# First-half retention: the last 128 queries of each head read a 384-token state in place of three score blocks

## The chip, the cores and the metric

The kernel runs on one core of a Trainium2 chip. The metric is the device time of one execution in microseconds (us). Before the change three runs took 1643.71, 1645.24 and 1647.24 us; their median, 1645.24, is the time before.

## The reference: what is computed

Two layers over 1024 tokens of width 1024, in float32. Layer 0 is a retention layer with 4 heads (queries and keys of 256 values, values of 512), layer 1 a stick-breaking attention. The change concerns the retention alone, for which the reference says, per head with decay gamma,

```
o_t = sum over s <= t of gamma^(t-s) (q_t . k_s) v_s
```

and which it computes in chunks of 128 tokens: scores inside a chunk, and a state (the decayed sum of k_j v_j^T over all earlier chunks, 256 x 512 values) for what lies ahead of the chunk. Each row of o is then normalised to mean 0 and variance 1 over its 512 values, multiplied by a gate and projected.

## The kernel before, in words

**Precision.** Each float32 operand is held as two numbers of the matmul format, a high part and the rest. `split` makes them: ACT copies the source (high part), DVE subtracts that copy from the source (low part). A product is a triple of matmuls, `mm3`: high x high, high x low, low x high. ACT, DVE and PE therefore see one, one and three instructions for each tile.

**Retention, tiled.** The tokens are two halves (t = 0 and 1) of 512, each four blocks of 128. The decay is put on values and normalisation constants when they are loaded, so that scores and states need no decay table. A unit `AHead(t, h)` is one head on one half. In `scores`, `fetch` loads q, k and v in eight loads and splits each; `score(jb)` multiplies key block jb with the queries from block jb on, 512, 384, 256 or 128 wide, in two halves of the 256 dimensions, so six matmuls into one PSUM tile `pz`; the result is split into `sc` and its diagonal block masked on POOL. For t = 0, `kt(tb)` also transposes the keys of a block (four PE transposes and one ACT copy, tile `vo`).

In `mix`, `o(ib)` sums, for query block ib, one triple for each key block up to it (tile `po`), then takes statistics on DVE, three small operations on POOL and one normalising ACT operation (`sgn`) that reads `po` last; that ACT operation of block ib is issued with block ib + 1. For t = 0, `state_out(d)` multiplies the transposed keys of all four blocks with the values (four triples for each half d of the dimensions), scales, splits (`ko`) and stores the state; for t = 1, `state_in` loads it and each o starts with two triples of queries with state. `gate` multiplies with the gate and transposes.

**Tiles and order.** PSUM has eight banks: two each for `pma`, `pmb`, `pz` and `po`. SBUF tiles of like size share groups of buffers: `b` (28 buffers; among them `ko`, `v` and the wide scores) and `f` (25; raw weights `wraw`, `f`, `sg`, `vo` and the narrow scores). Nothing runs in the order in which it is written: `merge` interleaves a main list (projection chunks) with side lists (the scores of the next head, the mix of this one), every operation is recorded (line 229), and `Plan` then sets the order on each engine by a list schedule with costs for operations, loads and buffers. All loads and stores go through SP's queue, in order. The first half's head 0 runs beside the last chunks of the gate projection, heads 1 to 3 beside the output projection of the head before.

## Time and profile before

| | |
|---|---|
| median of three runs | 1645.24 us |
| the profiled execution | 1644.4 us, span 1642.7 us |
| PE busy | 1625.7 us (99% of the span), 7638 matmuls |
| DVE, ACT, POOL busy | 1259.9, 806.6, 253.1 us |
| mean granted PE clock | 0.998 |
| the first-half heads | from about 450 to 612 us of the span |

The times of a timeline row are its start from the beginning of the span and its length. A PE row's length includes the pipeline's drain, so rows overlap: what a group costs is the start of the next row less its own. Every operation has line 229 (the recorder), so tiles tell them apart: `pz`, `po`, `pma`, `pmb` are PSUM tiles, `whl` split weights, `wraw` weights as loaded, `ko` split q, k or state, `vo` transposed keys, `oT` and `qk` inputs of the output projection.

### The profile page before, as it was taken

To read this page: it belongs to the slowest core of one execution; us is meant where nothing else is said; L and a number is where in the kernel's file an instruction comes from. 1 tells how busy PE (TensorE), PEld (TensorE's weight loads), DVE (VectorE), ACT (ScalarE), POOL (GpSimd) and SP (SyncE) were. 2 spreads that over 40 slices of the span, in tenths; PEclk is the share of its full clock that TensorE was granted. 3 is DMA by queue.
4 is the path that set the end of the run, shared out by engine and by line. 5 is a ranking of instruction groups with operands and counts; after the bars stand their busy time and mean duration, and the time that the engine had idled before them with its cause. 6 is when DMAs were issued, how large, how long until landed. Compare 5 with 4: busy or idle time off the path is not lost.

```text
span 1642.7 us, 23070 instructions
## 1 busy us (share of the span) xinstructions
PE 1625.7 (99%) x7638; PEld 1351.8 (82%) x7638; DVE 1259.9 (77%) x1955; ACT 806.6 (49%) x1480; POOL 253.1 (15%) x339
## 2 busy tenths in 40 slices
PE   8999999999999999999999999999999999999997
PEld 7888888888888888888878888888888888888886
DVE  6998679795775667777999677756747887778997
ACT  7633432322665445533665454545555655545643
POOL 0000024230022113451300000000002221212510
PEclk9999999999999999999999999999999999999999
DMA  7675636486567787788667686657686878787894
GB/s 277 238 247 176 224 117 217 154 299 219 188 232 260 249 281 257 256 296 293 213 212 266 259 301 210 249 167 253 221 319 215 277 239 301 275 283 258 279 305 150
DMA packets 196824, 399.60 MB, mean 243 GB/s; under 512 B 22112, under 2 KB 22752, under 8 KB 196704
## 3 DMA queue, kind: packets, MB, share of 16 engines
q1 hardware_dynamic: 196704, 398.12, 70.5%
q8 instruction: 60, 0.98, 0.3%
q14 instruction: 60, 0.49, 0.1%
HBM read 282.69 MB, written 115.34 MB: 242 GB/s over the span
## 4 chain that ended last, share of the span: by engine, by line
PE 77%; DVE 2%; issue 1%; ACT 0%; POOLq 0%; DVEq 0%; POOL 0%
PE po L229 20%; PE pma L229 20%; PE pmb L229 20%; PE pz L229 17%; DVE f L229 1%; DVE S L229 0%; DVE whl L229 0%; DVE wraw L229 0%; DVE acc L229 0%; POOLq L1762 0%; DVEq L1762 0%; ACT qk L229 0%; POOL col L229 0%; ACT whl L229 0%; DVE small L229 0%
## 5 line engine op out<-in xcount | busy, mean ns | idle before, releaser
L229 ACT ACTIVATE whl<-wraw 128x512 fp32r<-128x512 f32 (+1 forms) x392 | 233.3, 626 | 312.4 <-PE pmb L229 105.0
L229 DVE TENSOR_TENSOR whl<-wraw,whl 128x512 fp32r<-128x512 f32 x392 | 281.8, 742 | 135.0 <-ACT whl L229 134.3
L229 PE MATMUL pmb<-oT,whl 128*128 128x512 f32 x552 | 142.9, 394 | 0.0
L229 PE MATMUL pma<-oT,whl 128*128 128x512 f32 x552 | 140.2, 394 | 0.0
L229 PE MATMUL pma<-whl,xh 128*128 128x512 f32 x456 | 118.5, 393 | 1.0 <-DVE whl L229 0.9
L229 PE MATMUL pmb<-whl,xh 128*128 128x512 f32 x456 | 118.0, 393 | 0.9 <-ACT f L229 0.9
L229 PEld LDWEIGHTS pma<-oT,whl 128*128 128x128 f32 x552 | 101.7, 188 | 20.4
L229 PEld LDWEIGHTS pmb<-oT,whl 128*128 128x128 f32 x552 | 101.2, 188 | 19.3
L229 POOL TENSOR_SCALAR_AFFINE_SELECT f<-f 128x128 f32<-128x128 f32 x64 | 31.3, 504 | 527.8 <-DMA wraw<-in_wts_dram 416.1
L229 PE MATMUL pz<-ko,ko 128*128 128x512 f32 (+3 forms) x480 | 103.9, 338 | 0.0
L229 PEld LDWEIGHTS pmb<-whl,xh 128*128 128x128 f32 x456 | 86.1, 189 | 19.9 <-ACT f L229 1.5
L229 PEld LDWEIGHTS pma<-whl,xh 128*128 128x128 f32 x456 | 85.6, 189 | 19.7 <-DVE whl L229 1.7
L229 PE MATMUL pma<-xh,whl 128*128 128x512 f32 x384 | 99.1, 392 | 0.0
L229 PE MATMUL pmb<-xh,whl 128*128 128x512 f32 x384 | 98.6, 390 | 0.0
L229 POOL TENSOR_TENSOR f<-f,f 128x512 f32<-128x512 f32 x32 | 51.0, 1604 | 253.7 <-DVE f L229 224.3
L229 PEld LDWEIGHTS pz<-ko,ko 128*128 128x128 f32 x480 | 78.4, 189 | 9.5 <-DVE AT L229 0.7
L229 PE MATMUL pz<-xh,whl 128*128 128x512 f32 x336 | 85.2, 389 | 0.0
L229 PE MATMUL po<-xh,whl 128*128 128x512 f32 x336 | 85.2, 389 | 0.0
L229 PEld LDWEIGHTS pmb<-xh,whl 128*128 128x128 f32 x384 | 71.8, 188 | 14.9
L229 PEld LDWEIGHTS pma<-xh,whl 128*128 128x128 f32 x384 | 71.4, 188 | 14.8 <-issue 0.2
L229 DVE SCALAR_TENSOR_TENSOR wraw<-wraw,gn,wraw 128x512 f32<-128x512 f32 x96 | 71.3, 757 | 14.3 <-ACT wraw L229 6.2
L229 ACT ACTIVATE AT<-pz 128x512 fp32r<-128x512 f32 (+1 forms) x96 | 45.9, 491 | 66.4 <-PE pz L229 64.9
(197 smaller groups left out, 3380.6 us busy)
## 6 DMA issues: line engine op xcount, KB each, us to landing
wraw<-in_wts_dram SPq DMA_DIRECT2D x559, 256.0 KB, 5.2
v<-v SPq DMA_DIRECT2D x64, 512.0 KB, 6.6
y<-f SPq DMA_DIRECT2D x112, 256.0 KB, 3.0
f<-y SPq DMA_DIRECT2D x88, 256.0 KB, 4.2
ko<-kq SPq DMA_DIRECT2D x40, 512.0 KB, 5.7
kq<-v SPq DMA_DIRECT2D x32, 512.0 KB, 6.0
av<-f SPq DMA_DIRECT2D x32, 256.0 KB, 2.7
ag<-sg SPq DMA_DIRECT2D x32, 256.0 KB, 2.7
```

The lines of the kernel that those rows point to most:

```text
L229: f(*[_real(a) for a in o.args], **{k: _real(v) for k, v in o.kw.items()})
```

## The change: what it does

For t = 0 the fourth query block (ib = 3) no longer multiplies with key blocks 0, 1 and 2. Scores lose those columns: widths 384, 256, 128 and 128 in place of 512, 384, 256 and 128. `kt` is now interleaved with `score`. After o(0), `state_part(d)` forms the state of blocks 0 to 2 (three triples a half), copies it to SBUF (`f`) and splits it (`ko`); o(3) takes two triples of queries with that state and one of its own scores. `state_out(d)` multiplies block 3 alone, adds the kept copy on DVE, then scales, splits and stores. The 256-wide and the 128-wide scores now share one tag in group `f`. The second half is as it was.

```diff
             def score(jb):
-                w = 512 - 128 * jb
+                w = 512 - 128 * jb if self.t else max(384 - 128 * jb, 128)
                 p = PS("z")
                 jl = slice(128 * jb, 128 * jb + 128)
                 for d in range(2):
-                    mm3(p[:, :w], k[d][:, 0, jl], k[d][:, 1, jl], q[d][:, 0, 128 * jb:], q[d][:, 1, 128 * jb:], d == 0, d == 1)
-                s = S(f"sc{jb}", [2, w], F32R)
+                    mm3(p[:, :w], k[d][:, 0, jl], k[d][:, 1, jl], q[d][:, 0, 128 * jb:128 * jb + w], q[d][:, 1, 128 * jb:128 * jb + w], d == 0, d == 1)
+                s = S(f"sc{jb}" if w > 256 else "sc2", [2, w], F32R)
...
-            st = [lambda jb=jb: score(jb) for jb in range(4)]
-            if self.t == 0:
-                st += [lambda tb=tb: kt(tb) for tb in range(4)]
-            return st
+            if self.t:
+                return [lambda jb=jb: score(jb) for jb in range(4)]
+            return [lambda f=f, b=b: f(b) for b in range(4) for f in (score, kt)]
...
+            def products(d, blocks):
+                p = PS("o")
+                for tb in blocks:
+                    n, kn, v = slice(128 * d, 128 * d + 128), self.kn[tb], self.v[tb]
+                    mm3(p[:], kn[:, 0, n], kn[:, 1, n], v[:, 0, :], v[:, 1, :], tb == blocks[0], tb == blocks[-1])
+                return p
+
+            def state_part(d):
+                p = products(d, (0, 1, 2))
+                f, s = S("f2", [512]), hl("ko")
+                A_.activation(f[:], p[:], AF.Copy)
+                split((s[:, 0, :], s[:, 1, :]), f[:])
+                self.part.append(f)
+                self.state.append(s)
 
             def state_out(d):
-                p = PS("o")
-                for tb in range(4):
-                    n, kn, v = slice(128 * d, 128 * d + 128), self.kn[tb], self.v[tb]
-                    mm3(p[:], kn[:, 0, n], kn[:, 1, n], v[:, 0, :], v[:, 1, :], tb == 0, tb == 3)
-                s = hl("ko")
-                gg = GAMMA[h] ** HT
-                A_.activation(s[:, 0, :], p[:], AF.Copy, scale=gg)
-                V.scalar_tensor_tensor(s[:, 1, :], p[:], gg, f32(s[:, 0, :]), ALU.mult, ALU.subtract)
+                p = products(d, (3,))
+                f, s = self.part[d], hl("ko")
+                V.tensor_tensor(f[:], p[:], f[:], ALU.add)
+                split((s[:, 0, :], s[:, 1, :]), f[:], GAMMA[h] ** HT)
                 dma(st_d[h][d][:], flat(s))
...
                 il = slice(128 * ib, 128 * ib + 128)
-                for d, s in enumerate(self.state):
+                blocks = range(ib + 1) if self.t or ib < 3 else (3,)
+                state = self.state if self.t or ib == 3 else []
+                for d, s in enumerate(state):
                     mm3(p[:], q[d][:, 0, il], q[d][:, 1, il], s[:, 0, :], s[:, 1, :], d == 0, False)
-                for jb in range(ib + 1):
+                for jb in blocks:
                     n = slice(128 * (ib - jb), 128 * (ib - jb) + 128)
                     sc, v = self.sc[jb], self.v[jb]
-                    mm3(p[:], sc[:, 0, n], sc[:, 1, n], v[:, 0, :], v[:, 1, :], not self.state and jb == 0, jb == ib)
+                    mm3(p[:], sc[:, 0, n], sc[:, 1, n], v[:, 0, :], v[:, 1, :], not state and jb == 0, jb == ib)
...
             if self.t == 0:
                 self.give = [lambda d=d: state_out(d) for d in range(2)]
-                return os
+                return os[:1] + [lambda d=d: state_part(d) for d in range(2)] + os[1:]
```

Where `Plan` puts this shows in the order on the engines. PE, head 0, before: o(2) (`po721`), o(3) (`po728`), two score groups of head 1, a projection chunk and the first state half (`po743`).

```order
L229 MATMUL po721_4516<-v651_4069,sc2664_4312 128x512 x3
L229 MATMUL po728_4539<-v647_4061,sc0660_4259 128x512 x3
L229 MATMUL po728_4539<-v649_4053,sc1662_4274 128x512 x3
L229 MATMUL po728_4539<-v651_4069,sc2664_4312 128x512 x3
L229 MATMUL po728_4539<-v653_4100,sc3666_4320 128x512 x3
L229 MATMUL pz736_4576<-ko684_4167,ko688_4182 128x256 x3
L229 MATMUL pz736_4576<-ko686_4175,ko690_4190 128x256 x3
```

PE, head 0, after, from the last triple of the second partial state (`po712`) to o(2)'s start; `pz715` and `pz717` are scores and transposed keys of head 1.

```order
L229 MATMUL po712_4454<-v651_4069,vo673_4334 128x512 x3
L229 MATMUL pz715_4441<-ko686_4250,ko690_4295 128x384
L229 MATMUL pz717_4482<-identr_69,ko688_4256 128x128
L229 MATMUL pz717_4482<-identr_69,ko690_4295 128x128
L229 MATMUL pz717_4482<-identr_69,ko688_4256 128x128
L229 MATMUL pz717_4482<-identr_69,ko690_4295 128x128
L229 MATMUL pma587_3834<-whl667_4197,xh176_1061 128x512 x3
L229 MATMUL pma588_3840<-whl667_4197,xh176_1061 128x512 x3
L229 MATMUL pmb589_3848<-whl667_4197,xh176_1061 128x512 x3
L229 MATMUL pmb590_3855<-whl667_4197,xh176_1061 128x512 x3
L229 MATMUL po719_4520<-v647_4053,sc0660_4240 128x512 x3
L229 MATMUL po719_4520<-v649_4061,sc2664_4284 128x512 x3
```

Score group and projection chunk stand between the partial state and o(1) (`po719`); o(2) follows with nine matmuls. Further down, PE, head 0, after: o(3) (`po734`) and the two completions of the state (`po749`, `po751`), the second of which takes o(3)'s bank.

```order
L229 MATMUL po734_4604<-ko711_4458,ko639_3983 128x512 x3
L229 MATMUL po734_4604<-ko714_4497,ko641_4041 128x512 x3
L229 MATMUL po734_4604<-v653_4100,sc2679_4384 128x512 x3
L229 MATMUL pmb589_3848<-whl699_4306,xh185_1144 128x512 x3
L229 MATMUL pmb590_3855<-whl699_4306,xh185_1144 128x512 x3
L229 MATMUL po749_4643<-v653_4100,vo681_4387 128x512 x3
L229 MATMUL pz753_4651<-ko684_4187,ko688_4256 128x128 x3
L229 MATMUL pz753_4651<-ko686_4250,ko690_4295 128x128 x3
```

Behind these stand four transposes, one matmul of `pma587`, and then `po751`. On ACT, after, the copies (`f2710`, `f2713`) and splits (`ko711`, `ko714`) of the partial state stand ahead of the fetch of head 2 (`ko771` and on), and the first copy behind a weight split (`whl746`).

```order
L229 ACTIVATE whl746_4430<-wraw747_4397 128x512
L229 ACTIVATE f2710_4446<-po709_4420 128x512
L229 ACTIVATE whl746_4430<-wraw748_4406 128x512
L229 ACTIVATE ko711_4458<-f2710_4446 128x512
L229 ACTIVATE sgn726_4472<-po702_4414,small708_4464,small707_4438 128x512
L229 ACTIVATE f2713_4484<-po712_4454 128x512
L229 ACTIVATE sc0716_4494<-pz715_4441 128x384
L229 ACTIVATE ko714_4497<-f2713_4484 128x512
L229 ACTIVATE vo718_4503<-pz717_4482 128x512
L229 ACTIVATE ko771_4509<-f2770_4461 128x512
```

The loads of `wraw747` and `wraw748` stand on SP's queue behind the store of a gate; before, those weights were loaded ahead of it.

## The prediction

> **What bounds the kernel now.** I read the page's busy shares first, then what the matmul engine waits for, then the stretch of the first-half heads.

> ```profile
> span 1642.7 us, 23070 instructions
> PE 1625.7 (99%) x7638; PEld 1351.8 (82%) x7638; DVE 1259.9 (77%) x1955; ACT 806.6 (49%) x1480; POOL 253.1 (15%) x339
> ```

> ```profile
> PE pma L229 <- ACT oT L229: 5.3, 1, 5.3
> PE pma L229 <- DVE whl L229: 0.9, 1, 0.9
> PE pmb L229 <- ACT f L229: 0.9, 1, 0.9
> PE pma L229 <- ACT qk L229: 0.8, 1, 0.8
> PE pz L229 <- DVE sgn L229: 0.5, 1, 0.5
> ```

> ```profile
> 450.00:610.00 160.00, 160.00 (x801) 134.46 (x800) 107.86 (x198) 85.89 (x153) 32.19 (x66) 1.00 0.76 255
> ```

> PE is busy for 99% of the span. The wait list holds five waits, 8.4 us in all; the last view, a row of the window table (columns: length, then PE, PEld, DVE, ACT, POOL busy, clock, DMA share, GB/s), covers the four first-half heads and shows PE busy for 160.00 of 160.00 us at clock 1.00. So there a matmul less is time less, and a wait added is time added. DVE is free for 52 us of the 160 and ACT for 74. The orders of all engines are the same, but for buffer numbers, up to 450 us and from about 612 us on, so what is won or lost in this stretch is carried to the end as a shift.

> **What goes: matmul time.** The price of one group of six score matmuls is the start of the next group less its own start (timeline of PE: start, length, work).

> ```profile
> 498.72 1.52 PE L229 MATMUL pz<-ko,ko 128*128 128x512 f32 x6
> 500.08 2.66 PE L229 MATMUL pma<-oT,whl 128*128 128x512 f32 x11
> 502.57 1.23 PE L229 MATMUL pz<-ko,ko 128*128 128x384 f32 x6
> 503.64 1.55 PE L229 MATMUL pmb<-oT,whl 128*128 128x512 f32 x6
> 505.03 2.21 PE L229 MATMUL po<-v,sc 128*128 128x512 f32 x9
> ...
> 511.16 0.88 PE L229 MATMUL pz<-ko,ko 128*128 128x256 f32 x6
> 511.87 2.91 PE L229 MATMUL pmb<-oT,whl 128*128 128x512 f32 x12
> 514.62 0.78 PE L229 MATMUL pz<-ko,ko 128*128 128x128 f32 x6
> 515.24 1.60 PE L229 MATMUL pma<-oT,whl 128*128 128x512 f32 x6
> 516.68 2.90 PE L229 MATMUL po<-v,vo 128*128 128x512 f32 x12
> ...
> 520.78 0.46 PE L229 MATMUL pz<-identr,ko 128*128 128x128 f32 x4
> 521.08 1.63 PE L229 MATMUL pma<-oT,whl 128*128 128x512 f32 x6
> ```

> Width 512: 500.08 - 498.72 = 1.36 us (0.227 each). 384: 503.64 - 502.57 = 1.07, and the six wide ones behind it take 1.39 in place of 1.36, so 1.10. 256: 0.71, and the twelve behind take 2.75 in place of 2.72, so 0.74. 128: 0.62, and the six behind take 1.44, so 0.70. Before, a head's scores are one of each: 3.90 us. After, widths 384, 256, 128, 128: 3.24. That is 0.66 less; the step from 256 to 128 columns gives only 0.04 of it, since a 128-wide matmul takes 103 ns here, hardly less than a 256-wide one at 118.

> [...]

> The output products go from 10 triples a head (1+2+3+4) to 9 (1+2+3, and 2 state + 1): three matmuls of 0.227, 0.68 us. The state's eight triples and the sixteen transposes a head (four take 521.08 - 520.78 = 0.30 us) are as many as before. A head saves 0.66 + 0.68 = 1.34 us, the four 5.36. Without the edge terms it is 0.74 + 0.68 = 1.42, or 5.7: the upper bound.

> **What is added off PE.**

> ```profile
> L229 ACT ACTIVATE ko<-po 128x512 fp32r<-128x512 f32 x8 | 4.8, 597 | 18.9 <-PE po L229 18.9
> L229 DVE TENSOR_TENSOR ko<-f,ko 128x512 fp32r<-128x512 f32 x9 | 6.1, 686 | 2.1 <-ACT ko L229 2.1
> L229 ACT ACTIVATE ko<-f 128x512 fp32r<-128x512 f32 x16 | 10.0, 632 | 7.6 <-DMA f<-aqk 7.5
> L229 DVE SCALAR_TENSOR_TENSOR ko<-po,ko 128x512 fp32r<-128x512 f32 x8 | 5.5, 687 | 15.8 <-ACT ko L229 15.8
> ```

> For each of two halves the partial state costs an ACT copy (597 ns, as `ko<-po`), an ACT split (632) and a DVE subtraction (686); its completion an addition on DVE (about 686) more than before, and its split reads SBUF instead of PSUM. A head adds four operations on each engine: about 2 x 1.28 = 2.6 us of ACT and 2 x 1.37 = 2.7 us of DVE (what the narrower score splits save is not counted). Over four heads some 10 us each, in 74 and 52 us of idle time: I count nothing, as long as PE does not wait for one of them. If all DVE additions were on the path, they would cost 11 us. There is no added DMA; the same stores and loads move by a few places on SP's queue.

> **The state's own chain.** From the last partial product to o(3) it is the copy, split and subtraction: 0.26 us until ACT starts (row below: twelve of the 24 end at 484.87), then 0.60 + 0.63 + 0.69, together 2.2 us. In the new order PE has, in head 0, a 384 matmul, four transposes, 12 + 6 + 9 wide matmuls, a 256 group, four transposes and 6 wide ones in between: 33 x 0.227 + 0.17 + 0.71 + 2 x 0.3 = 9.0 us; in the other heads more. Covered; without cover it would be 2.2 a head.

> ```profile
> 482.15 5.61 PE L229 MATMUL po<-v,vo 128*128 128x512 f32 x24
> ```

> ```profile
> 485.13 0.60 ACT L229 ACTIVATE ko<-po 128x512 fp32r<-128x512 f32 x1 [2.37 <-PE po L229]
> ```

> **The accumulators.** All o and state products share two PSUM banks, six uses a head before, eight after. A bank of an o block is free only when its normalisation has read it. Quoted: PE, DVE and ACT around o(3) of head 0.

> ```profile
> 478.04 1.50 PE L229 MATMUL pz<-ko,ko 128*128 128x256 f32 x12
> ```

> ```profile
> 478.24 0.70 DVE L229 BATCH_NORM_STATS2 small<-po 128x6 f32<-128x512 f32 x1
> ```

> ```profile
> 481.99 0.78 ACT L229 ACTIVATE sgn<-po,small,small 128x512 f32<-128x512 f32 x1 [0.78 <-POOL small L229]
> ```

> o(3) ends by 478.04 and its bank is read out at 482.77: 4.7 us, with other work queued between the steps. What the steps take by themselves is seen at o(0):

> ```profile
> 468.14 0.17 DVE L229 BATCH_NORM_AGGREGATE small<-small 128x2 f32<-128x6 f32 x1
> ```

> ```profile
> 468.40 0.19 POOL L229 TENSOR_TENSOR small<-small,cc 128x1 f32<-128x1 f32 x1 [10.64 <-DVE small L229]
> 468.67 0.56 POOL L229 TENSOR_TENSOR small<-small,mhalf 128x1 f32<-128x1 f32 x1
> 469.31 0.19 POOL L229 TENSOR_TENSOR small<-small,small 128x1 f32<-128x1 f32 x1
> ```

> 0.20 to the start, 0.70 for the statistics, 469.50 - 468.14 = 1.36 for the next four, 0.78 on ACT and about 0.1 between engines: near 3.2. In the new order of head 0 the second state completion takes o(3)'s bank after 6 + 3 wide matmuls, a 128 group, four transposes and one more: 10 x 0.227 + 0.70 + 0.3 = 3.3 us. So PE waits between 0 and 1.4 us there; I take 0.5, nearer the bare chain, because little else is queued on DVE by then. o(3) itself takes o(1)'s bank after 15 x 0.227 + 0.74 + 0.3 = 4.4 us, behind the eight ACT splits of the next head's fetch: 0 to 0.5, taken as 0.2. Behind a waiting PE stands the last projection chunk of the gates. In heads 1 to 3 twice as many projection matmuls lie between, and I count nothing.

> **The sum.** 5.36 - 0.5 - 0.2 = 4.7 us. The profiled execution's 1644.4 becomes 1639.7 and its span 1638.0; it is 0.8 under the median of the three runs, 1645.24, which becomes **1640.5 us** (-0.28%). About 0.2% (3.3 us) is what a measurement of this kernel can tell from no change.

> **Rivals.**

> *Waits eat the gain (0.17).* The bank waits come in full (1.4 + 0.5), and the first weights of head 0's output projection are late: they now stand on SP's queue behind a gate store instead of ahead of it, and their ACT split stands ahead of the copy that frees the first state bank.

> ```profile
> wraw<-in_wts_dram SPq DMA_DIRECT2D x559, 256.0 KB, 5.2
> ```

> At 5.2 us to land, that copy could be 1.3 us late. Saved: 5.36 - 1.9 - 1.3 = 2.2, time 1643.0. Against it: before, PE waits nowhere in this stretch.

> *The clock is throttled after such waits (0.06).*

> ```profile
> 822.38 0.98 PE L229 MATMUL pmb<-whl,xh 128*128 128x512 f32 x2 [0.88 <-ACT f L229]
> 824.30 0.97 PE L229 MATMUL pma<-whl,xh 128*128 128x512 f32 x3 [0.94 <-DVE whl L229]
> ```

> ```profile
> 825.00:830.00 5.00, 5.00 (x21) 4.19 (x20) 3.62 (x8) 0.70 (x2) 1.39 (x1) 0.66 0.98 338
> ```

> Two waits of 0.9 us two microseconds apart were followed by a mean clock of 0.66 for 5 us, a loss of 1.7. If head 0's waits do the same: 4.7 - 1.2 (waits in full) - 1.7 = 1.8 saved, 1643.4. The single 0.8 us wait on `qk` had no such sequel. [...]

> *More than the sum (0.11).* No wait at all and no edge terms, 5.7; or the shift takes the dip at 825 us out of the run, 1.7 more. Time 1639.5 to 1638.3.

> *Slower (0.06).* The partial state is not covered: its split stands on ACT behind the next head's eight fetch splits, which wait for their loads. Then o(3) has 2.2 + 5.1 (eight splits of 632 ns) + 5.2 (landing) = 12.5 us to wait for, against 9.0 of cover: 3.5 a head, 14.0 in all, 8.6 slower, 1653.8. It decides once the chain exceeds the cover by 1.34 in every head. Against it: in the new ACT order both splits stand ahead of the eight.

> **Chances.** The forecast 0.60, the others as above. Faster by over 0.2% means below 1641.95: the forecast, the better case and a tenth of the wait cases, less a little for the runs' own spread (1643.71 to 1647.24): 0.72. Within 0.2%: most of the two wait cases and that spread, 0.22. Slower 0.06. The range reaches from the better case, 1638.3, to the wait cases, 1643.4.

> **What would show it.** PE with 7626 matmuls (12 fewer) and about 5.4 us less of them between 450 and 612 us; head 0's waits on `po` at 0.7 us or less; DVE with 16 and ACT with 16 more operations; everything from 612 us on earlier by one amount. A PE wait of over 2 us there, a clock under 1.00, or a different shift at the end than at 612 us would make it wrong.

## The result and the profile after

The median went from 1645.24 us to **1641.96 us** (seven runs each; the changed kernel's from 1638.16 to 1642.45). The ratio is 0.9975, 95% interval 0.9965 to 0.9984, so 2.6 to 5.8 us faster. The forecast was 1640.5 (1638.3 to 1643.4). The profiled execution took 1640.3 us, its span 1638.6.

The page of the changed kernel: span and busy shares.

```profile
span 1638.6 us, 23061 instructions
PE 1621.8 (99%) x7626; PEld 1348.8 (82%) x7626; DVE 1263.4 (77%) x1971; ACT 814.1 (50%) x1496; POOL 257.8 (16%) x339
```

PE has 12 matmuls fewer, DVE and ACT 16 operations more each, as counted ahead. The waits of PE in the changed kernel (total, times, longest):

```profile
PE pma L229 <- ACT oT L229: 5.4, 1, 5.4
PE pma L229 <- DVE whl L229: 0.9, 1, 0.9
PE pmb L229 <- ACT f L229: 0.9, 1, 0.9
PE pma L229 <- ACT qk L229: 0.8, 1, 0.8
PE po L229 <- ACT sgn L229: 0.4, 1, 0.4
```

One wait is new, the last: a product in `po` waits for the normalisation (`sgn`) that frees its bank.

**Where the time went.** The two spans differ by 4.1 us, but that figure mixes the change with two things that lie elsewhere. The first-half heads can be measured alone, from their first score group to the first matmul of queries with state in the second half. I call this the stretch. Its two ends on PE, before and after:

```profile
449.80 1.52 PE L229 MATMUL pz<-ko,ko 128*128 128x512 f32 x6
...
616.07 0.68 PE L229 MATMUL po<-ko,ko 128*128 128x512 f32 x2
```

```profile
448.55 1.23 PE L229 MATMUL pz<-ko,ko 128*128 128x384 f32 x6
...
610.47 0.68 PE L229 MATMUL po<-ko,ko 128*128 128x512 f32 x2
```

The window table over exactly these stretches (length, then PE, PEld, DVE, ACT, POOL busy with their counts, clock, DMA share, GB/s), before and after:

```profile
449.80:616.07 166.27, 166.27 (x837) 139.82 (x836) 111.42 (x204) 88.14 (x157) 32.60 (x67) 1.00 0.76 256
```

```profile
448.55:610.47 161.92, 161.48 (x826) 135.56 (x824) 121.35 (x222) 97.27 (x176) 34.76 (x67) 1.00 0.77 264
```

The stretch went from 166.27 to 161.92 us: **the change is worth 4.35 us**, at a clock of 1.00 in both. PE idles for 0.44 us of it. DVE has 9.9 us more to do and ACT 9.1, and neither shows in the length.

The rest of the difference lies outside. The changed kernel was already 1.25 us ahead when the stretch began, mostly through one early wait that its profiled run did not have (the row of before at 55 us, and the same matmul after). Such a lead comes and goes: in ten of the twelve kernels profiled here PE has the same order up to the stretch, and it begins between 448.55 and 452.26 us.

```profile
55.14 0.50 PE L229 MATMUL pz<-sgn,onesr 128*128 128x512 f32 x1 [0.53 <-DVE sgn L229]
```

```profile
54.31 0.39 PE L229 MATMUL pz<-sgn,onesr 128*128 128x512 f32 x1
```

And it lost 1.5 us near 820 us, where the clock was halved for longer: the matmul behind the second wait there starts 5.59 us earlier than before (818.71 against 824.30), and from 832.37 us of before on all is earlier by 4.07 (828.30). The half clock, before and after:

```profile
825.80:829.22 3.42, 3.42 (x11) 2.74 (x11) 2.82 (x7) 0.70 (x2) 1.39 (x1) 0.50 0.99 333
```

```profile
818.61:825.43 6.82, 6.72 (x20) 5.65 (x21) 4.42 (x10) 1.43 (x4) 1.39 (x1) 0.50 0.97 305
```

So -1.25 - 4.35 + 1.5 = -4.1. The experiments below are read by the stretch first, since it is free of both; where two kernels have the same order in it, its length came out alike (161.92 here and in experiment seven, 160.07 and 160.05 in experiments six and ten). The timed medians follow in a table at the end.

### The profile page after: what moved, and what is told of

It reads as the page before. It is cut to its first block, busy times and chain, and to the rows that moved or that the text cites. A ratio compares the mean times of both kernels' runs of the same rounds, so it can differ in the third digit from the quotient of the medians.

```text
span 1638.6 us, 23061 instructions
## 1 busy us (share of the span) xinstructions
PE 1621.8 (99%) x7626; PEld 1348.8 (82%) x7626; DVE 1263.4 (77%) x1971; ACT 814.1 (50%) x1496; POOL 257.8 (16%) x339
## 4 chain that ended last, share of the span: by engine, by line
PE 98%; DVE 1%; issue 0%; DMA 0%; ACT 0%; POOL 0%; SPq 0%; POOLq 0%; DVEq 0%; ACTq 0%
PE pma L229 27%; PE pmb L229 26%; PE po L229 24%; PE pz L229 21%; DVE S L229 0%; DVE f L229 0%; DVE acc L229 0%; DMA S<-in_xT_dram 0%; DVE small L229 0%; SPq L229 0%; POOL small L229 0%; POOLq L1774 0%; ACT sgn L229 0%; DVE whl L229 0%; DVEq L1774 0%
## 5 line engine op out<-in xcount | busy, mean ns | idle before, releaser
L229 ACT ACTIVATE whl<-wraw 128x512 fp32r<-128x512 f32 (+1 forms) x392 | 233.4, 626 | 302.6 <-PE pmb L229 102.2
L229 DVE TENSOR_TENSOR whl<-wraw,whl 128x512 fp32r<-128x512 f32 x392 | 278.3, 733 | 133.5 <-ACT whl L229 133.0
L229 PE MATMUL pmb<-oT,whl 128*128 128x512 f32 x552 | 144.1, 395 | 0.0
L229 PE MATMUL pma<-oT,whl 128*128 128x512 f32 x552 | 139.8, 395 | 0.0
L229 PE MATMUL pma<-whl,xh 128*128 128x512 f32 x456 | 119.5, 396 | 0.9 <-DVE whl L229 0.9
L229 PE MATMUL pmb<-whl,xh 128*128 128x512 f32 x456 | 117.9, 393 | 0.9 <-ACT f L229 0.9
L229 PEld LDWEIGHTS pma<-oT,whl 128*128 128x128 f32 x552 | 101.7, 188 | 20.4
L229 PEld LDWEIGHTS pmb<-oT,whl 128*128 128x128 f32 x552 | 100.9, 188 | 19.0
L229 POOL TENSOR_SCALAR_AFFINE_SELECT f<-f 128x128 f32<-128x128 f32 x64 | 30.9, 498 | 528.3 <-DMA wraw<-in_wts_dram 416.4
L229 PEld LDWEIGHTS pmb<-whl,xh 128*128 128x128 f32 x456 | 86.2, 189 | 19.9 <-ACT f L229 1.5
L229 PEld LDWEIGHTS pma<-whl,xh 128*128 128x128 f32 x456 | 86.0, 190 | 19.8 <-DVE whl L229 1.6
L229 PE MATMUL pz<-ko,ko 128*128 128x512 f32 (+3 forms) x480 | 101.9, 332 | 0.0
L229 PE MATMUL pma<-xh,whl 128*128 128x512 f32 x384 | 99.1, 392 | 0.0
L229 PE MATMUL pmb<-xh,whl 128*128 128x512 f32 x384 | 98.6, 390 | 0.0
L229 POOL TENSOR_TENSOR f<-f,f 128x512 f32<-128x512 f32 x32 | 53.5, 1684 | 251.1 <-DVE f L229 210.1
L229 PE MATMUL po<-xh,whl 128*128 128x512 f32 x336 | 85.3, 389 | 0.0
L229 PE MATMUL pz<-xh,whl 128*128 128x512 f32 x336 | 85.3, 389 | 0.0
L229 PEld LDWEIGHTS pz<-ko,ko 128*128 128x128 f32 x480 | 77.3, 189 | 9.2 <-DVE AT L229 0.7
L229 PEld LDWEIGHTS pmb<-xh,whl 128*128 128x128 f32 x384 | 71.8, 188 | 14.9
L229 PEld LDWEIGHTS pma<-xh,whl 128*128 128x128 f32 x384 | 71.4, 188 | 14.8 <-ACT f L229 0.2
L229 DVE SCALAR_TENSOR_TENSOR wraw<-wraw,gn,wraw 128x512 f32<-128x512 f32 x96 | 71.1, 756 | 14.2 <-DMA wraw<-in_wts_dram 7.7
L229 ACT ACTIVATE AT<-pz 128x512 fp32r<-128x512 f32 (+1 forms) x96 | 45.9, 491 | 66.5 <-PE pz L229 64.8
## 6 DMA issues: line engine op xcount, KB each, us to landing
wraw<-in_wts_dram SPq DMA_DIRECT2D x559, 256.0 KB, 5.1
y<-f SPq DMA_DIRECT2D x112, 256.0 KB, 2.8
f<-y SPq DMA_DIRECT2D x88, 256.0 KB, 4.4
av<-f SPq DMA_DIRECT2D x32, 256.0 KB, 3.2
ag<-sg SPq DMA_DIRECT2D x32, 256.0 KB, 2.9
```

The lines of the kernel that those rows point to most:

```text
L229: f(*[_real(a) for a in o.args], **{k: _real(v) for k, v in o.kw.items()})
```

## The experiments

**One: what the score columns are worth.**

```diff
-                w = 512 - 128 * jb if self.t else max(384 - 128 * jb, 128)
+                w = 512 - 128 * jb
```

> The changed kernel, with the first half's scores computed again at the old widths (512, 384, 256, 128 columns per head); the extra columns are computed, split and not used, the rest is as changed. It prices the score part of the saving alone. Measure: the stretch on the matmul engine from the first score group of first-half head 0 to the first matmul of queries with state of the second half, 166.27 us before the change and 161.92 after. Theory (groups of six cost 1.36, 1.10, 0.74, 0.70 us at 512, 384, 256, 128): 0.66 a head more, so the stretch is 161.92 + 2.64 = 164.6, up to 0.4 less where the wider scores cover bank waits of head 0. [...] Rival, PE is not what sets the pace: no change, 161.9. In the whole time 2.6 us more than the changed kernel, 0.16% of it.

```profile
449.50:613.54 164.04, 164.04 (x825) 137.19 (x824) 122.11 (x221) 97.80 (x174) 35.73 (x67) 1.00 0.77 257
```

164.04 us, 2.12 more than the changed kernel and 0.16 below the range that was named (164.2 to 164.6). PE does not idle here at all (164.04 of 164.04), so the bank wait of head 0 is covered by the wider scores, and it is larger than the 0.4 allowed for it. Against experiment four, which has the narrow scores and no bank wait either (161.30), the columns cost 2.74, where 2.64 was worked out; the order on PE differs between the two, so a part of this can be the order's.

**Two: what the o products are worth.**

```diff
-                for jb in range(ib + 1):
+                for jb in range(0 if self.t or ib < 3 else 1, ib + 1):
...
-                    mm3(p[:], sc[:, 0, n], sc[:, 1, n], v[:, 0, :], v[:, 1, :], not self.state and jb == 0, jb == ib)
+                    mm3(p[:], sc[:, 0, n], sc[:, 1, n], v[:, 0, :], v[:, 1, :], not self.state and jb == (0 if self.t or ib < 3 else 1), jb == ib)
```

> The kernel before, with one of o(3)'s four triples left out in the first half (key block 0 is missing from the output of the last 128 queries of that half); scores, state and order of writing stay as before. It takes 12 wide matmuls out of the program and adds no chain of copies and no bank use: the saving of the o products alone, without the waits that come with the change. Theory (PE sets the pace, 0.227 us for each wide matmul): the stretch is 166.27 - 12 x 0.227 = 163.5, with no wait on po. Rival (the time is filled by waits for loads or for ACT): between 165.3 and 166.3. The whole time is 2.7 us below the kernel before, 0.17%.

```profile
451.41:615.04 163.63, 163.63 (x826) 137.58 (x824) 110.92 (x204) 88.57 (x157) 33.52 (x67) 1.00 0.77 262
```

163.63 us: 2.64 less than before, 0.220 for each of the 12 matmuls. Together the two parts are 2.64 + 2.74 = 5.38 us of matmul time. The sum in the prediction had 5.36, from 2.72 and 2.64: the products were put 0.08 too high and the columns 0.10 too low, and that the two errors cancel is luck.

**Three: is the state's chain covered?**

```diff
-                split((s[:, 0, :], s[:, 1, :]), f[:])
+                for _ in range(3):
+                    split((s[:, 0, :], s[:, 1, :]), f[:])
```

> The changed kernel with the partial state split three times in place of once (same values written again). This adds four ACT and four DVE operations a head, 2.5 and 2.7 us, and lengthens the chain from the last partial product to o(3) from 2.2 to about 4.9 us. Theory (that chain has 9.0 us of matmul work as its cover, and ACT and DVE have over 50 us free in the stretch): the stretch stays within 0.4 of 161.92, PE waits for no ko. Rival (the added ACT and DVE work is on the path): 2.6 a head more, 10 us in all, and already the change itself paid for half of that.

```profile
448.59:610.50 161.91, 161.73 (x825) 135.55 (x824) 130.86 (x238) 105.90 (x192) 36.70 (x67) 1.00 0.79 265
```

ACT has 8.6 us more, DVE 9.5, and the stretch is 161.91 in place of 161.92. So nearly as much work again as the change puts on ACT and DVE adds no net time. It is not without effect on the spot: o(1)'s normalisation comes later, and PE now waits ahead of o(3). The second completion, which `Plan` here puts behind two projection matmuls more, no longer waits, and at 487 us this kernel is 0.25 us ahead of the changed one; near 566 us, behind the transposes of the gated output, it loses that again. That the two stretches agree to 0.01 is thus chance; that 18 us of added work cost no more than some tenths is not.

```profile
479.30 1.65 PE L229 MATMUL po<-ko,ko 128*128 128x512 f32 x6 [0.18 <-ACT sgn L229]
```

**Four: the bank wait of head 0.** Both completions of the state are written ahead of o(3).

```diff
-                self.give = [lambda d=d: state_out(d) for d in range(2)]
-                return os[:1] + [lambda d=d: state_part(d) for d in range(2)] + os[1:]
+                self.give = []
+                out = [lambda d=d: state_out(d) for d in range(2)]
+                return os[:1] + [lambda d=d: state_part(d) for d in range(2)] + os[1:3] + out + os[3:]
```

> The changed kernel with both state completions written ahead of o(3) in the first half, so that the second completion no longer takes o(3)'s bank just after o(3). The work is the same. Theory (0.9 us of head 0's saving went to bank waits on po, some 0.7 to 0.8 of it to the second completion, which waits for o(3)'s normalisation): the 0.4 us wait of po on sgn goes from the wait list, head 0 is 0.7 to 0.8 shorter, the stretch is 161.1 to 161.3. Rival 1 (the 0.9 us are not a bank wait but matmuls that run longer or a late operand): the stretch stays at 161.9. Rival 2 (o(3) is later by two triples, its normalisation now holds up the gate's transposes or a bank of head 1): a wait of 0.5 us or more appears at pz or po, and the stretch is 161.9 or more.

The place in the changed kernel (PE; the last row is the second completion):

```profile
480.50 0.84 PE L229 MATMUL po<-v,sc 128*128 128x512 f32 x3
...
484.19 0.46 PE L229 MATMUL pma<-whl,xh 128*128 128x512 f32 x1
485.09 0.96 PE L229 MATMUL po<-v,vo 128*128 128x512 f32 x3 [0.44 <-ACT sgn L229]
```

The same place in this version, where o(3) follows the completions and takes a bank that a quick addition on DVE has freed (0.68 us, as timed at 483.47 us in the changed kernel):

```profile
483.18 0.84 PE L229 MATMUL po<-v,vo 128*128 128x512 f32 x3
...
484.81 0.46 PE L229 MATMUL pma<-whl,xh 128*128 128x512 f32 x1
485.12 1.53 PE L229 MATMUL po<-ko,ko 128*128 128x512 f32 x6
```

```profile
450.53:611.83 161.30, 161.30 (x825) 135.51 (x824) 120.55 (x221) 96.21 (x175) 33.65 (x67) 1.00 0.78 264
```

The step from the single `pma` matmul to the next row is 0.90 us in the changed kernel and 0.31 here. The stretch is 161.30, 0.62 shorter, where 0.6 to 0.8 was expected; no later wait took its place. The cause of the wait is shown.

**Five and six: the same idea one block further, in two orders of writing.** The core of the edit:

```diff
-                w = 512 - 128 * jb if self.t else max(384 - 128 * jb, 128)
+                w = 512 - 128 * jb if self.t else max(256 - 128 * jb, 128)
...
-                p = products(d, (0, 1, 2))
+                p = products(d, (0, 1))
...
+            def state_more(d):
+                p = products(d, (2,))
+                f, s = self.part[d], hl("ko")
+                V.tensor_tensor(f[:], p[:], f[:], ALU.add)
+                split((s[:, 0, :], s[:, 1, :]), f[:])
+                self.state.append(s)
...
-                blocks = range(ib + 1) if self.t or ib < 3 else (3,)
-                state = self.state if self.t or ib == 3 else []
+                blocks = range(ib + 1) if self.t or ib < 2 else (ib,)
+                state = self.state if self.t else {2: self.state[:2], 3: self.state[2:]}.get(ib, [])
...
-                return os[:1] + [lambda d=d: state_part(d) for d in range(2)] + os[1:]
+                return os[:1] + [lambda d=d: state_part(d) for d in range(2)] + os[1:2] + [lambda d=d: state_more(d) for d in range(2)] + os[2:]
```

> The changed idea carried one block further: in the first half o(2) also reads a state (blocks 0 and 1) in place of two score blocks, and o(3) reads that state completed by block 2. Scores are 256, 128, 128, 128 wide; the completion by block 2 is written after o(1). By the prices of the prediction the scores of a head cost 0.74 + 3 x 0.70 = 2.84 us in place of 3.24, the o products stay at nine triples: 0.40 a head, 1.6 in all. Each head adds 2.6 us of ACT and DVE and two more uses of the two banks. Theory (bank waits cost where an o block's bank is wanted again within about 3.2 us of matmul work): the second completion by block 2 takes o(1)'s bank after some 2.7 us, so 0.5 us a head is lost again; stretch 160.3 to 162.3. Rival (PE work alone decides): 161.92 - 1.6 = 160.3. Rival (ACT and DVE become the bound): above 163.

```profile
452.26:613.67 161.41, 160.55 (x825) 134.10 (x824) 129.22 (x238) 101.17 (x185) 33.93 (x67) 1.00 0.77 264
```

161.41 lies in the range, but the mechanism was another. There is no bank wait in every head. PE idles 0.86 us, once, at the end of head 0, where the gate and the transposed output (`oT`) come late to the output projection:

```profile
492.77 1.25 PE L229 MATMUL pz<-ident,sgn 128*128 128x128 f32 x8 [0.17 <-DVE oT L229]
494.71 0.50 PE L229 MATMUL pma<-oT,whl 128*128 128x512 f32 x1 [0.69 <-ACT oT L229]
```

With the completions ahead of o(1) and o(3):

```diff
-                self.give = [lambda d=d: state_out(d) for d in range(2)]
-                return os[:1] + [lambda d=d: state_part(d) for d in range(2)] + os[1:2] + [lambda d=d: state_more(d) for d in range(2)] + os[2:]
+                self.give = []
+                part, more, out = ([lambda f=f, d=d: f(d) for d in range(2)] for f in (state_part, state_more, state_out))
+                return os[:1] + part + more + os[1:3] + out + os[3:]
```

> The same work as the kernel with two states, in another order of writing: both completions by block 2 ahead of o(1), both completions by block 3 ahead of o(3), so that no state product takes the bank of an o block just computed. Theory (0.9 of head 0's loss are bank waits, 0.62 of which went when the completions were written ahead of o(3)): stretch 161.30 - 1.6 = 159.7, no wait on po over 0.2 us. Rival (the longer chain of copies, additions and splits is no longer covered): PE waits on ko ahead of o(2), 0.5 us a head or more, stretch 161.5 or more.

```profile
448.72:608.79 160.07, 160.04 (x825) 134.02 (x824) 129.50 (x237) 101.52 (x184) 32.60 (x67) 1.00 0.78 267
```

160.07 against an expected 159.7: the second state brought 1.23 us over experiment four and not the 1.6 of the prices. PE idles 0.03 us; the order of writing is worth 1.3 us with the same work, most of it at the end of head 0, where PE no longer waits for `oT`. DVE is at 129.5 of 160 us, so the second state's additions are hidden too.

**Seven and eight: the clock dip near 820 us.** It differs between the two profiled runs, so it bears on how this change is measured. One kernel relieves DVE where the waits ahead of the dip stand, one moves that place.

```diff
-                (V if t else G).tensor_tensor(box["acc"][:], box["acc"][:], raw[:], ALU.add)
+                G.tensor_tensor(box["acc"][:], box["acc"][:], raw[:], ALU.add)
```

> The changed kernel with one edit outside the retention: at the end of layer 0, second half, the eight additions that sum the squares run on POOL instead of DVE. It tests whether the clock dip near 820 us (0.86, 0.50 and 0.96 in three windows of 5 us, 3.4 us lost, in the changed kernel; 1.7 lost in one window of 0.66 before) comes from the two waits of 0.88 and 0.94 us that stand there behind ACT and DVE. DVE has 8 x 0.69 = 5.5 us less to do between 803 and 820. Theory (waits cause the dip): if the two waits go or fall under 0.5 us, no window there has a clock below 1.00, and the kernel is 1.8 us of waits and up to 3.4 us of clock faster. Rival (the clock drops by itself some 809 to 816 us after it first reached full speed): the dip stays without the waits. If the waits only move, nothing is told apart. Up to 610 us nothing changes: stretch 161.9.

The waits there became 0.34 and 1.41 us, and the dip was one step:

```profile
815.13 0.50 PE L229 MATMUL pmb<-whl,xh 128*128 128x512 f32 x1 [0.34 <-ACT f L229]
817.04 1.61 PE L229 MATMUL pma<-whl,xh 128*128 128x512 f32 x4 [1.41 <-DVE whl L229]
```

```profile
817.60:821.01 3.41, 3.41 (x10) 2.63 (x8) 3.41 (x4) 0.00 (x0) 2.14 (x2) 0.50 0.97 322
```

The waits did not go, so by its own terms this run tells nothing of the cause. Its median is lower than the changed kernel's, but the intervals of the two ratios overlap (table).

```diff
-                blocks = range(ib + 1) if self.t or ib < 3 else (3,)
+                blocks = (ib,)
```

> The changed kernel with only the diagonal score block left in each o product of both halves (the scores of earlier blocks are computed and not used; the output lacks them). It takes 9 triples a head out, 108 wide matmuls, 24.5 us: 36 of them, 8.2 us, in the first-half stretch, the rest before 770 us. It moves the two waits near 817 us ahead to about 792. Theory (the waits cause the clock dip): the dip moves with them and begins at 792 to 799 us. Rival (the clock drops by itself 809 to 816 us after it first reached full speed, 9 to 14 us into the run): the dip stays at 818 to 830 us. Stretch: 161.9 - 8.2 = 153.7 if PE sets the pace; more where shorter o products cover bank waits less, up to 1.5 a head.

```profile
450.35:603.42 153.07, 153.07 (x790) 128.74 (x788) 120.25 (x221) 96.83 (x175) 33.96 (x67) 1.00 0.81 275
```

```profile
799.89 1.83 PE L229 MATMUL pz<-ones,acc 128*128 128x1 f32 x8 [5.71 <-DVE acc L229]
```

```profile
796.62:806.86 10.24, 6.97 (x21) 5.84 (x22) 8.91 (x17) 6.10 (x12) 1.45 (x1) 0.50 0.87 304
```

The dip went with PE's waits to 796.62 us, and with one long wait of 5.71 us in place of two short ones it lasted 10.24 us. That does not yet exclude a clock that drops by itself after a fixed time, since the long wait can have lowered it on its own; the last section compares all kernels. The stretch is 153.07, 8.85 shorter, 0.6 below the expected 153.7: 36 x 0.227 = 8.17, and 0.68 that is about the bank wait of head 0, which is gone here (PE is busy for 153.07 of 153.07).

**Nine: one part of the change alone.** The kernel before, with the transposed keys written between the scores.

```diff
-            st = [lambda jb=jb: score(jb) for jb in range(4)]
-            if self.t == 0:
-                st += [lambda tb=tb: kt(tb) for tb in range(4)]
-            return st
+            if self.t:
+                return [lambda jb=jb: score(jb) for jb in range(4)]
+            return [lambda f=f, b=b: f(b) for b in range(4) for f in (score, kt)]
```

> The kernel before, with one part of the change alone: each block's transposed keys are written right behind its scores in the first half, in place of behind all four. The work is the same. It tells where the rest of the lost gain is: the parts priced 2.64 (one triple left out) and 2.74 (old score widths against the version without the bank wait) make 5.38 us, the version without the bank wait gained 4.97. Theory (interleaving makes more changes from a narrow matmul to a 512-wide one, 39 in place of 31 in the stretch, at 0.06 us each): the stretch is 0.3 to 0.5 longer than 166.27. Rival (the interleaving is free and the rest lies in the banks or in the order of the o products): 166.2 to 166.4.

```profile
449.61:616.08 166.47, 166.47 (x837) 139.72 (x836) 111.39 (x204) 87.91 (x157) 33.20 (x67) 1.00 0.77 259
```

0.20 us longer than before: less than the 0.3 to 0.5 of the theory, and a little past the rival's 166.2 to 166.4. The theory is not the cause: counted in the trace, this kernel has 31 changes from a narrower matmul to a 512-wide one, as many as before (the changed kernel has 40). The 0.20 lies in head 0, ahead of 495 us; its cause stays open. This run also shows something on the dip: the waits ahead of it are those of the kernel before to 0.02 us (0.88 and 0.94 at 822.38 and 824.30 there), yet the half clock lasted twice as long.

```profile
822.39 0.98 PE L229 MATMUL pmb<-whl,xh 128*128 128x512 f32 x2 [0.86 <-ACT f L229]
824.31 1.07 PE L229 MATMUL pma<-whl,xh 128*128 128x512 f32 x3 [0.94 <-DVE whl L229]
```

```profile
825.01:831.84 6.83, 6.83 (x22) 5.77 (x21) 3.62 (x8) 0.69 (x2) 1.39 (x1) 0.50 0.97 337
```

**Ten: six and seven together** (two states with the completions ahead, squares on POOL).

> The two edits that paid, together: two states with all completions written ahead (stretch 160.07 us) and the sum of squares at the end of layer 0 on POOL (the clock dip there was one step of 3.41 us at half speed in place of two). Theory: stretch 160.1; one dip step near 818 us or none; span 1636.0 (the run with the squares on POOL) - 1.85 (161.92 - 160.07) = 1634.2, within the 1.3 us by which start-up and the early wait differ from run to run. Rival (the dip has two steps again, since its length hangs on how the waits fall in the clock's own steps): 1.7 more, 1635.9.

```profile
449.52:609.57 160.05, 160.03 (x825) 134.06 (x824) 129.51 (x237) 100.91 (x184) 34.03 (x67) 1.00 0.79 267
```

```profile
816.99 1.19 PE L229 MATMUL pma<-whl,xh 128*128 128x512 f32 x4 [1.40 <-DVE whl L229]
```

```profile
800.00:850.00 50.00, 48.27 (x211) 38.42 (x210) 47.09 (x67) 34.09 (x64) 12.83 (x9) 1.00 0.59 205
```

The stretch is 160.05, as expected (160.1). With the waits of experiment seven (1.40 us here, 1.41 there) there is no dip at all in this execution. The span of 1634.4 meets the expected 1634.2 by luck: that figure still had one step of half clock in it, and the 1.7 us that it would have cost were lost ahead of the stretch, which begins at 449.52 here and at 447.70 in experiment seven. By the median it is the fastest of the kernels that compute the whole result.

| kernel | stretch, us | median, us | ratio to before (95%) |
|---|---|---|---|
| before | 166.27 | 1645.24 | |
| changed | 161.92 | 1641.96 | 0.9975 (0.9965 to 0.9984) |
| 1 old score widths | 164.04 | 1643.09 | 0.9985 (0.9976 to 0.9995) |
| 2 before, a triple left out | 163.63 | 1643.02 | 0.9984 (0.9975 to 0.9994) |
| 3 state split three times | 161.91 | 1641.10 | 0.9975 (0.9964 to 0.9985) |
| 4 completions ahead of o(3) | 161.30 | 1641.04 | 0.9976 (0.9966 to 0.9986) |
| 5 two states | 161.41 | 1641.30 | 0.9982 (0.9972 to 0.9991) |
| 6 two states, completions ahead | 160.07 | 1639.09 | 0.9969 (0.9957 to 0.9982) |
| 7 squares on POOL | 161.92 | 1638.68 | 0.9966 (0.9954 to 0.9977) |
| 8 diagonal blocks alone | 153.07 | 1622.96 (one run) | |
| 9 before, keys between scores | 166.47 | 1646.09 (one run) | |
| 10 six and seven together | 160.05 | 1636.96 | 0.9949 (0.9936 to 0.9963) |

Each ratio is to executions of the kernel before that were timed together with it. By their intervals the medians part the kernels only in the large: the changed kernel is not told apart from any of one to seven by them, but is from one, two, four, five and six by the stretch (one execution each). Ten is told apart from it by both.

## Why the prediction was right, and where it was off

The direction, the size and the mechanism held: 4.7 us forecast, 4.35 in the stretch, 3.3 between the medians with an interval of 2.6 to 5.8 by the ratio. The size is in part luck: two errors in the matmul sum cancel, and the losses, put at 0.7, were 5.38 - 4.35 = 1.03.

- **PE sets the pace in the stretch.** Right. Matmuls taken out come back as time at 0.220 us each (experiment two), and 18 us of ACT and DVE work added there cost no net time (three).
- **The matmul time that goes, 5.36.** Right as a sum, 2.64 + 2.74 = 5.38 by experiments two and one; by parts, the products were 2.64 in place of 2.72 and the columns 2.74 in place of 2.64.
- **Added ACT and DVE work, counted at nothing.** Right in both halves: about 10 us each were foreseen, 9.9 and 9.1 were measured, hidden.
- **The state's chain, 2.2 us against 9.0 of cover.** Right as far as it was tried: three splits in place of one leave the stretch as it is, and PE waits for no `ko`. The slower rival, which rested on this chain, falls.
- **The second completion's bank wait, 0.5.** Right in place and mechanism, a little small: the step behind the matmul at 484.19 is 0.90 us in place of 0.31, and experiment four got 0.62 back. The cover of 3.3 us was right; the bare chain of 3.2 was too short a measure. In the changed kernel o(3)'s last product starts at 480.50 + 2 x 0.227 = 480.95; DVE starts its statistics at 481.38, and the bank is read out at 485.04. Counted as in the prediction, from the start of the next row (481.18), the chain is 3.86 us. POOL's two steps in it, 0.19 and 0.56 us at o(0), took 0.56 and 0.94:

```profile
482.38 0.56 POOL L229 TENSOR_TENSOR small<-small,cc 128x1 f32<-128x1 f32 x1 [1.16 <-DVE small L229]
483.01 0.94 POOL L229 TENSOR_TENSOR small<-small,mhalf 128x1 f32<-128x1 f32 x1
...
484.04 0.19 POOL L229 TENSOR_TENSOR small<-small,small 128x1 f32<-128x1 f32 x1
```

```profile
484.26 0.78 ACT L229 ACTIVATE sgn<-po,small,small 128x512 f32<-128x512 f32 x1 [2.22 <-POOL small L229]
```

- **o(3)'s bank wait, 0.2.** It did not come in the changed kernel: o(3) starts 479.12 - 477.67 = 1.45 us behind the start of six wide matmuls that follow a narrow group, where 1.44 is the price without a wait.

```profile
477.67 1.62 PE L229 MATMUL pma<-whl,xh 128*128 128x512 f32 x6
479.12 1.54 PE L229 MATMUL po<-ko,ko 128*128 128x512 f32 x6
```

- **What the sum lacked.** 5.38 - 0.62 = 4.76, and 4.35 came, so 0.41 is missing, as in experiment four (166.27 - 161.30 = 4.97). Some 0.1 of it lies at the second partial product: its nine matmuls last 2.17 us up to the next row, where 2.04 would do (0.03 of this is the usual edge behind a 384-wide group). It takes the bank of the first partial product, since o(0)'s is read by `sgn` only from 468.69 on, and its first weight load waits for the ACT copy that empties that bank. This handover, of a bank use that the change adds, was left out of the sum. The other 0.3 is not shown. The changed kernel has nine more changes from a narrower to a 512-wide matmul than before (40 and 31), at up to 0.08 each, of which the group prices hold four (the 128-wide group that each head adds); experiment nine's 0.20, which comes without such changes, may be in it too, but `Plan`'s order differs there.

```profile
467.81 2.33 PE L229 MATMUL po<-v,vo 128*128 128x512 f32 x9
469.98 0.34 PE L229 MATMUL pz<-ko,ko 128*128 128x384 f32 x1
```

```profile
467.81 1.91 PEld L229 LDWEIGHTS po<-v,vo 128*128 128x128 f32 x9 [0.20 <-ACT f L229]
```

```profile
467.15 0.60 ACT L229 ACTIVATE f<-po 128x512 f32<-128x512 f32 x1 [1.57 <-PE po L229]
```

- **The weights of the output projection.** The rival in which the first copy of the state is 1.3 us late for them, a figure given without its working, did not happen: that copy starts at 467.15 (row above), 0.26 us behind the last product at 466.89, and PE has no wait on `whl` in the stretch. Nor was the clock throttled there (1.00).
- **One amount from 612 us to the end.** Wrong, and named as what would make the prediction wrong. The lead was 5.60 us at the end of the stretch and 4.1 at the end of the span. The step that failed is the assumption that all else runs as in the execution at hand: the time ahead of the stretch and the length of the dip at 820 us differ from one execution to the next, by up to 3.7 us (448.55 to 452.26) and by steps of 3.41 us at half clock, some 1.7 us of time each, whatever the change. The single profiled execution of before had the shorter dip.
- **The range's lower end, 1638.3.** It does not follow from the better case's own terms: 5.7 saved gives 1639.5, and 1.7 more than the forecast gives 1638.8. Nothing above rests on it.

## What to carry to other kernels

Where one engine is busy for all of a stretch at full clock, price a change by that engine's start-to-start times and then look for what the change adds to scarce buffers: here each of the two matmul terms was right to 0.1 us, and 1.0 us was lost on the way, 0.7 of it at two bank handovers. A product whose bank is freed by a long chain (3.86 us behind o(3) here) should not be followed soon by a use of the same bank; writing the quickly freed ones (one addition of 0.68 us) next to it gave 0.62 us in experiment four. A change of a few tenths of a per cent is read better from the length of the stretch that it touches than from spans.

## What the runs showed of the hardware

In these runs the dip went with the waits, not with a fixed time. By the clock records of the traces PE first had its full clock 8.2 to 13.8 us into the span (before 10.01, the changed kernel 9.65). From there to the dip it took 808.96 us in seven kernels, 812.37 in experiment one, 815.79 before and in nine, and 785.07 in eight; in ten there was no dip near 820 us. These are 237, 238, 239 and 230 steps of 3.4133 us, and the dip of before is recorded with 3.413. The first of the two waits stands 805.6 to 806.8 us behind the start of the full clock in the seven, 809.9 in experiment one, 811.5 before and 812.3 in nine. The dip follows the waits, then, and began in each of these runs at the first end of a step behind the start of the second wait (in eight, of the one long wait).

Where the steps' ends fall may bear on it. In experiment seven both waits lie in one step; in ten nearly the same waits are cut by a step's end at 816.34, if the steps are counted on from the start of the full clock (an estimate, 10.80 + 236 x 3.4133), and no dip came. PE's busy time in a step is the figure behind its length:

```profile
814.18:817.60 3.42, 1.67 (x6) 0.86 (x5) 3.42 (x4) 3.15 (x6) 2.79 (x2) 1.00 0.99 341
```

```profile
812.93:816.34 3.41, 2.33 (x10) 1.35 (x8) 3.41 (x5) 3.39 (x7) 2.61 (x2) 1.00 0.82 306
816.34:819.75 3.41, 2.76 (x12) 2.31 (x13) 3.41 (x3) 0.95 (x2) 3.25 (x3) 1.00 0.99 336
```

It does not decide alone. Before, a step's end parts the two waits as well, 2.47 us of the step ahead of the dip are busy, and a dip of one step came; and experiments seven and nine, busy for 1.67 and 1.68 us of the step ahead, had one step and two. When a step is lost and for how long stays open. A wait of 0.88 us and one of 0.94, with PE at work between them, were enough for one step before and for two in the changed kernel.

A step costs up to 1.7 us (3.41 us at half clock), half of the 3.3 between the medians. How much of the spread of the timed runs it makes up was not shown: the seven of the changed kernel have mean clocks of 0.997 and 0.998.
